# The first load of x in two transfers, one of 16 partitions and one of the other 112, in a fused residual add and layer normalisation

## The chip, the cores and the metric

One core of a Trainium2 chip. The metric is the time of one execution on the device in microseconds (us), the median of several. The profile's span is 1.3 us shorter than the time of the same run (236.7 for 238.0 us before).

Some terms: SBUF is the on-chip memory, with 128 partitions. A load is cut into packets, here one for each partition that it writes, and 16 DMA engines move them; it has landed when each of the 16 has reported its share (so 144 packets for a load of all partitions: the trace of before has 4464 for 31 transfers, 496 of them of 4 bytes). A row, of a load, is what it writes in one partition: one packet.

## The reference

```python
# x, residual: (16, 1024, 512) float32; gamma, beta: (512,)
z = x + residual
mean = np.mean(z, axis=-1, keepdims=True)
var = np.var(z, axis=-1, keepdims=True)
return gamma * (z - mean) / np.sqrt(var + eps) + beta
```

That is 16384 rows of 512 numbers; 33.55 MB each of x, of the residual and of the result.

## The kernel before

Every partition holds 128 of the rows. The plan names the transfers in the order in which the SP queue issues them: x0+8 is rows 0 to 7 of each partition, 16 KB per partition. POOL adds x and the residual in place, ACT takes mean and variance, DVE normalises into the buffer of x, and SP stores from there.

```python
PLAN = """
x0+8 r0+8 x8+8 r8+8 x16+16 r16+16 x32+16 r32+16 x48+16
o0+16 r48+16 o16+16 x64+16 ...
"""
EARLY = 2
# ... cut ...
def dram(t, lo, n):                 # 128 pieces of n rows, 32 KB apart in memory
    b0 = lo - lo % BLOCK
    v = t[P * b0 : P * (b0 + BLOCK), :].rearrange("(p j) d -> p j d", p=P)
    return v[:, lo - b0 : lo - b0 + n, :].rearrange("p a b -> p (a b)")
# ... cut ...
def move(out, in_, s):
    i = nc.sync.dma_start(out=out, in_=in_).then_inc(s, 16)
    if len(first) < EARLY:
        first.append(i.ins)         # these are put ahead of the start-up barrier
# ... cut: for each word of the plan ...
        if kind == "x":
            # ... wait for the store that frees the place ...
            move(part(zbuf, Z_ROWS, lo, n), dram(xf, lo, n), sx[loads_x.index((lo, n))])
# ... cut: POOL ...
            while landed[key] < len(loads) and loads[landed[key]][0] < lo + n:
                nc.gpsimd.wait_ge(s[landed[key]], 16)
```

## Time and profile before

| | before |
|---|---|
| time, median of the first 3 runs | 238.26 us (238.25 to 238.43) |
| span of the profile | 236.7 us |
| DMA queue's packets, share of 16 engines' span | 99.4% |
| ACT, DVE, POOL busy | 78%, 75%, 61% |
| one 16 KB packet, undisturbed | 0.611 us |
| first add starts | 12.29 us |

The first row carries the result, the third says what bounds it: 16 DMA engines whose packets fill 99.4% of the span. The lines behind this table are shown in the prediction.

### The profile page before, as it was taken

To read this page: it belongs to the slowest core of one execution; us is meant where nothing else is said; L and a number is where in the kernel's file an instruction comes from. 1 tells how busy PE (TensorE), PEld (TensorE's weight loads), DVE (VectorE), ACT (ScalarE), POOL (GpSimd) and SP (SyncE) were. 2 spreads that over 40 slices of the span, in tenths; PEclk is the share of its full clock that TensorE was granted. 3 is DMA by queue.
4 is the path that set the end of the run, shared out by engine and by line. 5 is a ranking of instruction groups with operands and counts; after the bars stand their busy time and mean duration, and the time that the engine had idled before them with its cause. 6 is when DMAs were issued, how large, how long until landed. Compare 5 with 4: busy or idle time off the path is not lost.

```text
span 236.7 us, 1000 instructions
## 1 busy us (share of the span) xinstructions
PE 3.8 (2%) x4; PEld 1.2 (0%) x4; DVE 177.2 (75%) x290; ACT 183.8 (78%) x545; POOL 144.0 (61%) x36
## 2 busy tenths in 40 slices
PE   0600000000000000000000000000000000000000
PEld 0100000000000000000000000000000000000000
DVE  0001999629999999599980999809999999999950
ACT  2019997299999996999909998099999999999600
POOL 0098920999799307993079920899799798800000
DMA  8999999999999999999999999999999999999997
GB/s 310 443 426 432 426 443 443 443 443 443 410 388 443 443 443 432 426 393 432 443 443 443 443 438 421 415 421 432 429 424 435 426 432 440 439 432 443 438 390 324
DMA packets 4469, 100.68 MB, mean 425 GB/s; under 512 B 498, under 2 KB 498, under 8 KB 500
## 3 DMA queue, kind: packets, MB, share of 16 engines
q1 hardware_dynamic: 4464, 100.67, 99.4%
q14 instruction: 1, 0.01, 0.0%
q10 hardware_dynamic: 4, 0.00, 0.0%
HBM read 67.11 MB, written 33.55 MB: 425 GB/s over the span
## 4 chain that ended last, share of the span: by engine, by line
ACT 48%; DMA 35%; POOL 6%; DVE 4%; issue 1%; SPq 1%; ACTq 0%; DVEq 0%; POOLq 0%
DMA rbuf<-in_residual_dram 35%; ACT junk_s L211 25%; ACT junk_m L201 21%; POOL rbuf L178 6%; DVE zbuf L239 3%; ACT std L220 2%; DVE zbuf L253 1%; SPq L140 1%; DVE rstd L247 0%; ACTq L194 0%; DVEq L231 0%; POOLq L175 0%; ACTq L199 0%; ACTq L195 0%
## 5 line engine op out<-in xcount | busy, mean ns | idle before, releaser
L178 POOL TENSOR_TENSOR rbuf<-zbuf,rbuf 128x2048 f32<-128x2048 f32 x32 | 143.7, 4521 | 62.2 <-DMA rbuf<-in_residual_dram 60.0
L239 DVE SCALAR_TENSOR_TENSOR zbuf<-rbuf,nm,gamma_p 128x512 f32<-128x512 f32 x128 | 87.1, 743 | 47.8 <-ACT std L220 47.8
L201 ACT ACTIVATE junk_m<-rbuf 128x512 f32<-128x512 f32 x128 | 74.2, 580 | 34.0 <-POOL rbuf L178 33.7
L211 ACT ACTIVATE junk_s<-rbuf,nm 128x512 f32<-128x512 f32 x128 | 88.8, 694 | 1.0
L253 DVE SCALAR_TENSOR_TENSOR zbuf<-zbuf,rstd,beta_p 128x512 f32<-128x512 f32 x128 | 87.1, 744 | 1.1
L211 ACT ACTIVATION_READ_ACCUMULATOR junk_s<-rbuf,nm 128x1 f32 x128 | 23.9, 187 | 0.0
L201 ACT ACTIVATION_READ_ACCUMULATOR junk_m<-rbuf 128x1 f32 x128 | 23.8, 186 | 0.0
L220 ACT ACTIVATE std<-ssq,eps_t 128x4 f32<-128x4 f32 x32 | 9.5, 297 | 1.0
L247 DVE RECIPROCAL rstd<-std 128x4 f32<-128x4 f32 x32 | 5.5, 171 | 0.0
L192 ACT ACT_TABLE_LOAD x1 | 1.3, 1283 | 2.7 <-PEq L60 2.7
L131 PE MATMUL gamma_p<-gb_row,ones 1*128 1x512 f32 x2 | 2.0, 1122 | 6.6 <-DMA gb_row<-in_gamma_dram 6.6
L131 PE MATMUL beta_p<-gb_row,ones 1*128 1x512 f32 x2 | 1.9, 1056 | 0.0
L126 DVE MEMSET ones<- 1x128 f32 x1 | 0.2, 165 | 2.0 <-PEq L60 2.0
L131 PEld LDWEIGHTS beta_p<-gb_row,ones 1*128 1x128 f32 x2 | 0.7, 332 | 1.0 <-DMA gb_row<-in_beta_dram 0.5
L131 PEld LDWEIGHTS gamma_p<-gb_row,ones 1*128 1x128 f32 x2 | 0.5, 306 | 6.6 <-issue 6.6
L294 POOL MEMSET const-float32-0.0<- 128x1 f32 x1 | 0.1, 98 | 0.2 <-issue 0.2
L294 POOL MEMSET const-bfloat16-1.0<- 128x1 bf16 x1 | 0.1, 101 | 0.0
L294 POOL MEMSET const-uint8-127<- 128x1 uint8 x1 | 0.1, 101 | 0.0
L294 POOL MEMSET const-float32-1.0<- 128x1 f32 x1 | 0.1, 98 | 0.0
L127 DVE MEMSET eps_t<- 128x1 f32 x1 | 0.1, 59 | 0.0
## 6 DMA issues: line engine op xcount, KB each, us to landing
zbuf<-in_x_dram SPq DMA_DIRECT2D x6, 4096.0 KB, 28.9
rbuf<-in_residual_dram SPq DMA_DIRECT2D x6, 4096.0 KB, 21.2
out_dram<-zbuf SPq DMA_DIRECT2D x6, 4096.0 KB, 31.0
zbuf<-in_x_dram SPq DMA_DIRECT2D x4, 2048.0 KB, 14.9
rbuf<-in_residual_dram SPq DMA_DIRECT2D x4, 2048.0 KB, 14.0
out_dram<-zbuf SPq DMA_DIRECT2D x3, 2048.0 KB, 22.5
out_dram<-zbuf SPq DMA_DIRECT2D x2, 1024.0 KB, 10.0
gb_row<-in_gamma_dram ACTq DMA_DIRECT2D x1, 2.0 KB
```

The source lines that it names most:

```text
L126: nc.vector.memset(ones[:, :], 1.0).then_inc(s_const, 1)
L131: nc.tensor.matmul(dest[:, :], ones[:, :], gb_row[:, k * D : (k + 1) * D], start=True, stop=True).then_inc(s_pe, 1)
L140: i = nc.sync.dma_start(out=out, in_=in_).then_inc(s, 16)
L178: nc.gpsimd.tensor_tensor(out=z, in0=part(zbuf, Z_ROWS, lo, n), in1=z, op=ALU.add).then_inc(s_sum[lo // TURN % R_TURNS], 1)
L192: act.preload_act_table_set("sqrt_and_others")
L201: i = act.activation(out=junk_m[k][:, :], in_=part(rbuf, R_ROWS, r, 1), func=ACT.Identity, scale=-inv_d, accum_out=column(nm, r),)
L211: i = act.activation(out=junk_s[k][:, :], in_=part(rbuf, R_ROWS, r, 1), func=ACT.Square, bias=column(nm, r), accum_out=column(ssq, r),)
L220: act.activation(out=column(std, rows[0], TURN), in_=column(ssq, rows[0], TURN), func=ACT.Sqrt, bias=eps_t[:, 0:1], scale=inv_d,).then_inc ...
L239: dve.scalar_tensor_tensor(out=part(zbuf, Z_ROWS, r, 1), in0=part(rbuf, R_ROWS, r, 1), scalar=column(nm, r), in1=gamma_p[:, :], op0=ALU.ad ...
L247: dve.reciprocal(out=column(rstd, rows[0], TURN), in_=column(std, rows[0], TURN)).then_inc(s_rstd[j], 1)
L253: i = dve.scalar_tensor_tensor(out=z, in0=z, scalar=column(rstd, r), in1=beta_p[:, :], op0=ALU.mult, op1=ALU.add,)
L294: nc = _bacc.Bacc("TRN2", target_bir_lowering=False, num_devices=1)
```

## The change

Its intent is not written down; its shape suggests one: a first transfer of 16 partitions would give each of the 16 DMA engines one row at once, so that all start early.

```diff
+AHEAD = 16
...
-            move(part(zbuf, Z_ROWS, lo, n), dram(xf, lo, n), sx[loads_x.index((lo, n))])
+            cuts = (0, AHEAD, P) if lo == 0 else (0, P)
+            for a, b in zip(cuts, cuts[1:]):
+                move(
+                    part(zbuf, Z_ROWS, lo, n)[a:b, :],
+                    dram(xf, lo, n)[a:b, :],
+                    sx[loads_x.index((lo, n))],
+                )
...
-                nc.gpsimd.wait_ge(s[landed[key]], 16)
+                twice = key == "x" and landed[key] == 0
+                nc.gpsimd.wait_ge(s[landed[key]], 32 if twice else 16)
```

Since EARLY stays 2, both pieces of x go ahead of the barrier and the first residual load behind it.

## The prediction

The sum came to 1.83 + 0.2 - 0.25 + 0.01 = +1.8 us, so 240.06, and 239.9 us with a little off for the rivals. The 1.83 of step 4 is three more row times of 0.611 us: the author assumed that a first row takes four of them if the 16 rows go to partitions 0 to 15. The 0.2 of step 5 is a guess between nothing and one row time more for the seven rows of each engine. The 0.15 of step 3 is a guess from the measured spread of 0.47 us. In the paragraph on range and chances, 239.6 to 240.8 us, and the word contention, stand for the losses of steps 4 and 5.

> **What bounds the kernel now.** I read the summary by slices first, because the change touches only a load and the question is whether loads are the bound at all. In the page of the kernel before, the rows of section 2 for the DMA engines and their rate, the rows of section 3, and the bytes:
>
> ```profile
> DMA  8999999999999999999999999999999999999997
> GB/s 310 443 426 432 426 443 443 443 443 443 410 388 443 443 443 432 426 393 432 443 443 443 443 438 421 415 421 432 429 424 435 426 432 440 439 432 443 438 390 324
> q1 hardware_dynamic: 4464, 100.67, 99.4%
> HBM read 67.11 MB, written 33.55 MB: 425 GB/s over the span
> ```
>
> The 16 DMA engines are busy from the first slice to the last (each slice is 236.7/40 = 5.9 us), and the queue's packets fill 99.4% of the 16 engines' span. No compute engine comes near: DVE 75%, ACT 78%, POOL 61%. The chain of waits names ACT for 48% of the span, but every long wait of POOL in it ends on a load, and ACT waits on POOL. What matters is that ACT's waits cost the DMA engines nothing: the queue never runs dry.
>
> Then the packet records of the trace. The kernel moves 100.66 MB, 6.29 MB for each engine, or 384 rows of 16 KB. An undisturbed 16 KB packet takes 611 ns (26.8 GB/s per engine, 429 GB/s for 16), one of 32 KB 1213 ns. All packets of q1 together, divided by 16, are 235.2 us. The first packet starts at 1.02 us and the last one ends at 236.1, its landing following at 236.6. So there is next to no idle time after the start: **the span is the start, plus the packets' time, plus about half a microsecond of last landing.** Anything that makes the DMA engines lose time at the start moves the end by the same amount, since nothing later has slack on that side; anything that moves only compute does not.
>
> The stretches of the beginning, with DMA share and GB/s as the last two columns (bytes are put down to where a packet starts, so the first stretches are lumpy):
>
> ```profile
> 0.00:1.00 1.00, 0.00 (x0) 0.00 (x0) 0.00 (x0) 0.00 (x0) 0.20 (x4) 1.00 0.00 0
> 1.00:1.50 0.50, 0.00 (x0) 0.00 (x0) 0.00 (x0) 0.00 (x0) 0.00 (x0) 1.00 2.47 524
> 1.50:2.00 0.50, 0.00 (x0) 0.00 (x0) 0.00 (x0) 0.00 (x0) 0.00 (x0) 1.00 0.00 0
> 2.00:2.50 0.50, 0.00 (x0) 0.00 (x0) 0.17 (x2) 0.00 (x0) 0.00 (x0) 1.00 0.90 360
> 3.00:4.00 1.00, 0.00 (x0) 0.00 (x0) 0.00 (x0) 0.99 (x1) 0.00 (x0) 1.00 1.01 426
> ```
>
> Nothing moves in the first microsecond; the 16 first packets, one per engine, start between 1.02 and 1.49 (mean 1.20), last 1.02 to 1.37 us instead of 0.611, and end at 2.43 on average. From there each engine runs one packet per 0.61 us. The whole possible gain is in this corner: the 0.2 us by which the mean start trails the first one, and the 0.6 us by which each first packet is too long.
>
> The issues on the SP queue, from the timeline:
>
> ```profile
> 0.00 0.38 SPq L140 DMA_DIRECT2D zbuf<-in_x_dram  x1
> 0.43 0.42 SPq L140 DMA_DIRECT2D rbuf<-in_residual_dram  x1
> 1.92 0.33 SPq L140 DMA_DIRECT2D zbuf<-in_x_dram  x1
> 12.29 8.95 POOL L178 TENSOR_TENSOR rbuf<-zbuf,rbuf 128x2048 f32<-128x2048 f32 x2 [11.85 <-DMA rbuf<-in_residual_dram]
> ```
>
> Two issues stand ahead of the start-up barrier; the next is at 1.92. The first add waits for the residual's load until 12.29, long after x's own (last share at 7.31 us).
>
> [...]
>
> **The change part by part.**
>
> 1. *One issue more, and order.* The instruction listing of the changed kernel shows that only SP's list differs, with 31 rows for 30. The two transfers ahead of the barrier are now both of x; the first residual load moves behind the barrier. It is issued near 1.92 instead of 0.43, and everything behind it slips by one issue, 0.33 to 0.51 us. x's rows keep each engine occupied until about 6.7 us (mean end of the first packet 2.43 + 7 x 0.611), so a residual issue at 1.92 with about 1.0 us to its first packet is ready by 3: nothing starves. Cost 0. One more transfer also means 16 more completion packets of 9 ns, one per engine: 0.01 us.
>
> 2. *POOL's wait for 32 instead of 16*: same wait, ends when both landed. Cost 0.
>
> 3. *Earlier first packets.* [...] the mean start moves from 1.20 to about 1.05: a gain of 0.15 us, 0.4 at most for the last-starting engine. The first start itself, 1.02 after the issue's beginning, may move forward if it waits for the whole issue (0.38 us), by up to 0.3; I give that a third and count 0.1. Gain about 0.25.
>
> 4. [...] each first packet ends 1.83 us later, near 4.25 less the gain of step 3, so 4.0. [...] Cost 1.83 us.
>
> 5. [...] a further 0 to 0.6 us, partly hidden as engines that are ahead go on to the residual. I count 0.2.
>
> Sum: 1.83 + 0.2 - 0.25 + 0.01 = +1.8 us on the DMA path and, as the path has no slack, on the time: 238.26 + 1.8 = 240.06. I take a little off for rivals below: **239.9 us**.
>
> **The rivals.**
>
> *The early start wins.* [...] only step 3 is left: 237.8 to 238.2. For it speaks the shape of the change: 16 is just the number that gives each engine one row, as somebody would choose who knows the engine count. [...] I give it 20%.
>
> *Hidden anyway.* The first add doesn't need x before 12.29, and x lands at 7.31. A delay of x alone would be hidden from compute. But the residual's packets stand in the same engines behind x's, and the bound is the DMA queue, not compute. For "same to 0.1 us" the two effects would have to cancel: 10%.
>
> *A poor split of 112.* If 112 rows ran on eight engines (14 rows each), these would have 8.6 us of work; six rows more than before are 3.7 us late on half the engines[...]. Then 242 to 244. [...] 4%.
>
> *Late residual.* If the residual's issue slipped to beyond 5 us through the barrier, the engines would run dry. It would take 3 us more than the 1.92 seen; nothing in the change touches the barrier.
>
> **Range and chances.** [...] 239.6 to 240.8 (step 4 less step 3 alone is +1.6, with the whole of step 5 +2.2, and 0.2 for the spread of runs); contention of half the size 239.0; the early start alone 238.0. Eight times in ten: 238.0 to 240.8. 2% is 4.77 us; no rival but the poor split comes near, and the largest possible gain is the idle 1.02 us and the 0.6 us of slow first packets, under 2%. So faster 0.005, within 97.5%, slower 0.02.
>
> **What would show it.** In the changed kernel's packet records, the first 16 packets should last about 3.0 us and not 1.2, and end near 4.0; x's last share should land near 9 instead of 7.3, the first add start near 14 instead of 12.29, the first slice fall from 310 GB/s to about 190 (1.8 us x 429 GB/s = 0.77 MB less, over 5.9 us), and all other slices keep their rates. The first starts should lie within 0.2 us. Step 4 is wrong if the first packets stay under 1.6 us; step 1 if a gap opens on the DMA engines before 7 us; step 5 if packets of the second transfer stay at 0.611 throughout or run far over it. The prediction as a whole fails if the first add comes earlier than 12.29 and the time falls below 238.

## More of the kernel before

One more view is needed for the comparison, the beginning in stretches of 2 us (columns: stretch and length, busy time and instructions of PE, PEld, DVE, ACT, POOL, granted clock, DMA share, GB/s), of the kernel before:

```profile
0.00:2.00 2.00, 0.00 (x0) 0.00 (x0) 0.00 (x0) 0.00 (x0) 0.20 (x4) 1.00 0.62 131
2.00:4.00 2.00, 0.00 (x0) 0.00 (x0) 0.17 (x2) 1.28 (x1) 0.00 (x0) 1.00 0.94 393
4.00:6.00 2.00, 0.00 (x0) 0.00 (x0) 0.00 (x0) 0.00 (x0) 0.00 (x0) 1.00 0.95 402
6.00:8.00 2.00, 1.37 (x2) 0.83 (x3) 0.00 (x0) 0.00 (x0) 0.00 (x0) 1.00 1.08 460
8.00:10.00 2.00, 2.00 (x3) 0.33 (x1) 0.00 (x0) 0.00 (x0) 0.00 (x0) 1.00 1.05 451
```

From 2 us on the rate is that of the whole run (425 GB/s); a packet's bytes count where it starts, so single stretches lie a little over or under.

## The result, and the profile after

241.6 us (241.32 to 241.71, 4 runs) against 238.28 us before: ratio 1.0137 (95% interval 1.0122 to 1.0152). A ratio is the mean time of one kernel's fast runs over that of the other's in the same rounds, so it is not quite the ratio of the medians quoted. The time lies outside the range of 238.0 to 240.8 us, and the loss of 3.3 us is twice the 1.6 us forecast. The direction was right, the place half right, the size wrong.

The page of the changed kernel, the rows that answer to those in the prediction:

```profile
GB/s 197 323 431 421 464 437 437 431 431 437 421 426 410 437 421 431 437 437 437 437 437 437 437 431 426 437 431 421 412 431 426 431 429 442 433 437 437 437 393 311
q1 hardware_dynamic: 4480, 100.67, 99.3%
HBM read 67.11 MB, written 33.55 MB: 419 GB/s over the span
```

The first two slices carry the loss: 197 for 310 and 323 for 443 GB/s. The first one alone is near what was forecast (190 is written there; the sum beside it, 0.77 MB over 5.9 us off 310, gives 179); the second one was to stay as it was. In microseconds of the engines' full rate of 429 GB/s: (310 - 197) x 5.9 us / 429 = 1.55 us in the first, (443 - 323) x 6.0 / 429 = 1.68 us in the second, together 3.2. The DMA queue is as "busy" as before, 99.3%: **a packet counts as busy for as long as it lasts**, at 0.9 to 1.7 us as at 0.61, so the share can't show this loss, only the rate can.

The same stretches of 2 us in the changed kernel:

```profile
0.00:2.00 2.00, 0.00 (x0) 0.00 (x0) 0.00 (x0) 0.00 (x0) 0.20 (x4) 1.00 0.68 139
2.00:4.00 2.00, 0.00 (x0) 0.00 (x0) 0.17 (x2) 1.28 (x1) 0.00 (x0) 1.00 0.98 172
4.00:6.00 2.00, 0.00 (x0) 0.00 (x0) 0.00 (x0) 0.00 (x1) 0.00 (x0) 1.00 0.98 279
6.00:8.00 2.00, 0.00 (x0) 0.00 (x0) 0.00 (x0) 0.00 (x0) 0.00 (x0) 1.00 1.10 312
8.00:10.00 2.00, 0.51 (x1) 0.50 (x2) 0.00 (x0) 0.00 (x0) 0.00 (x0) 1.00 1.01 280
10.00:12.00 2.00, 2.00 (x3) 0.61 (x2) 0.00 (x0) 0.00 (x0) 0.00 (x0) 1.00 0.89 377
12.00:14.00 2.00, 1.24 (x2) 0.00 (x0) 0.00 (x0) 0.00 (x0) 0.00 (x0) 1.00 0.96 410
14.00:16.00 2.00, 0.00 (x0) 0.00 (x0) 0.00 (x0) 0.00 (x0) 0.13 (x1) 1.00 1.02 434
```

There are two parts: one stretch at 172 GB/s, then six microseconds at 279 to 312, and from about 11 us the full rate again. The packet records put figures to it. Sorted by start in groups of 16, one packet for each engine, the mean durations are (us):

| packet of each engine | 1 | 2 | 3 | 4 | 5 | 6 | 7 | 8 | 9 | 10 |
|---|---|---|---|---|---|---|---|---|---|---|
| before | 1.23 | 0.64 | 0.63 | 0.62 | 0.63 | 0.61 | 0.61 | 0.61 | 0.61 | 0.61 |
| after | 1.24 | 1.68 | 0.99 | 0.92 | 0.86 | 0.91 | 0.94 | 0.97 | 0.92 | 0.62 |

The first is as long as before, the second 1.04 us longer, the third to ninth 2.19 us longer in sum. Together 3.2 us, which is the loss. By count, the first packet of each engine is of the 16 rows, the next seven are of the 112, and the ninth is of the residual. A landing comes about one packet after the last packet's end in these records: x0 landed at 7.31 us in before, where the eighth packets end at 6.76 on average and the ninth at 7.38, and the 16 rows at 4.25 in the changed kernel, where the first packets end at 2.39 and the second at 4.08. So a slow row seems to show one packet late, and the second packet is read here as the price of the 16 rows and the third to ninth as that of the 112, which experiments 7 and 10 measure apart. The timeline and the landings of the changed kernel (issue to landing, by size):

```profile
0.00 0.86 SPq L143 DMA_DIRECT2D zbuf<-in_x_dram  x2
1.92 0.35 SPq L143 DMA_DIRECT2D rbuf<-in_residual_dram  x1
15.87 4.49 POOL L188 TENSOR_TENSOR rbuf<-zbuf,rbuf 128x2048 f32<-128x2048 f32 x1 [15.43 <-DMA rbuf<-in_residual_dram]
```

```profile
zbuf<-in_x_dram SPq DMA_DIRECT2D x1, 1792.0 KB, 10.5
zbuf<-in_x_dram SPq DMA_DIRECT2D x1, 256.0 KB, 4.3
```

The 16 rows, 256 KB, need 4.3 us to land, the other 112 are there at 10.9 us (all of x0 at 7.3 before), the first add starts 3.6 us later, and everything after it is shifted as a whole: the last store lands 3.3 us later.

### The profile page after: what moved, and what is told of

Its sections match the earlier page's. It is cut to its first block, busy times and chain, and to the rows that moved or that the text cites. A ratio compares the mean times of both kernels' runs of the same rounds, so it can differ in the third digit from the quotient of the medians.

```text
span 240.0 us, 1001 instructions
## 1 busy us (share of the span) xinstructions
PE 3.7 (2%) x4; PEld 1.1 (0%) x4; DVE 177.2 (74%) x290; ACT 183.8 (77%) x545; POOL 144.0 (60%) x36
## 3 DMA queue, kind: packets, MB, share of 16 engines
q1 hardware_dynamic: 4480, 100.67, 99.3%
## 4 chain that ended last, share of the span: by engine, by line
ACT 48%; DMA 36%; POOL 6%; DVE 4%; issue 1%; SPq 1%; ACTq 0%; DVEq 0%; POOLq 0%
DMA rbuf<-in_residual_dram 36%; ACT junk_s L221 25%; ACT junk_m L211 21%; POOL rbuf L188 6%; DVE zbuf L249 3%; ACT std L230 2%; DVE zbuf L263 1%; SPq L143 1%; DVE rstd L257 0%; ACTq L204 0%; DVEq L241 0%; POOLq L185 0%; ACTq L209 0%; ACTq L205 0%
```

## The experiments

P is the theory that the loss lies in which partitions are written: rows to some sets of partitions, here called crowded, hold each other up (collide, in the expectations), rows to others don't. Its rivals name the number or the size of the transfers, the start, the barrier and the reading side. Which sets are crowded, and by how much, the author assumed before each run from a layout that no run of this case shows. P's figures (mostly the first ones given) read as bets. Each edit is given against the changed kernel ("after") or the kernel before; the times of before are those of the same rounds.

**1. Is it the residual load that left the opening?** Against after:

```diff
-EARLY = 2
+EARLY = 3
```

> The changed kernel with three transfers ahead of the barrier instead of two, so that the first residual load is again issued at about 1 us and not at 1.92. [...] no change, 241.6 us, first sixteen packets 1.2 us, the others of x0 0.8 to 1.05 us. Rival, the residual load that left the opening is the cost: back to about 238.3 us.

Measured: 241.3 us against 238.13, ratio 1.0144 (1.0127 to 1.0161). The residual is issued at 0.90 us, ahead of the barrier again, and nothing is won; second packets 1.70 us, the next 0.79 to 1.03. The rival falls.

**2 and 3. Cuts of the same kind on other partitions.** Against after, for 64+64 `AHEAD = 64`; for 32+64+32:

```diff
-            cuts = (0, AHEAD, P) if lo == 0 else (0, P)
+            cuts = (0, 32, 96, P) if lo == 0 else (0, P)
...
-                nc.gpsimd.wait_ge(s[landed[key]], 32 if twice else 16)
+                nc.gpsimd.wait_ge(s[landed[key]], 48 if twice else 16)
```

> The first load cut at partition 64, four rows per engine in each piece. [...] all eight rows take 1.22 us instead of 0.611: 8 x 0.61 = 4.9 us more, 243.2 us. Rival, that it is the small piece of 16 or the odd number 7 of rows that costs: 238.3 to 238.6 us, packets at 0.611. Rival, a fixed cost per further transfer: 241.6.

> The first load in three pieces: partitions 0-31, 32-95, 96-127. [...] 4 x 0.61 = 2.4 us more, 240.7 us, less than the two pieces of 64 although there is one transfer more. Rival, number of transfers or size of the pieces: more than 64+64, or twice the change's 3.3 us, 244.9 us.

Measured: 64+64 243.0 us, ratio 1.0207 (1.019 to 1.0224), +4.9 us as expected, though the exact agreement is partly luck: 0.47 us of it is a later start (the first packets start at 1.67 us on average, for 1.20), and the packets themselves lose 4.4; 32+64+32 240.38 us, ratio 1.0099 (1.0083 to 1.0116), +2.3 us (the bet was 1.22 us a row in the outer pieces, two rows per engine in each, and 0.611 in the middle one). The three pieces cost half of the two. Stretches of the kernel with 64+64, then of that with 32+64+32:

```profile
2.00:4.00 2.00, 0.00 (x0) 0.00 (x0) 0.17 (x2) 0.71 (x1) 0.00 (x0) 1.00 1.08 238
4.00:6.00 2.00, 0.00 (x0) 0.00 (x0) 0.00 (x0) 0.57 (x1) 0.00 (x0) 1.00 0.84 172
8.00:10.00 2.00, 0.00 (x0) 0.00 (x0) 0.00 (x0) 0.00 (x0) 0.00 (x0) 1.00 1.00 206
```

```profile
2.00:4.00 2.00, 0.00 (x0) 0.00 (x0) 0.17 (x2) 0.88 (x1) 0.00 (x0) 1.00 1.15 254
4.00:6.00 2.00, 0.00 (x0) 0.00 (x0) 0.00 (x0) 0.41 (x1) 0.00 (x0) 1.00 0.82 336
8.00:10.00 2.00, 1.95 (x2) 0.50 (x2) 0.00 (x0) 0.00 (x0) 0.00 (x0) 1.00 0.85 254
```

The middle lines matter most: at 4 to 6 us both kernels have a 64-partition transfer in flight, four rows per engine (64 rows on 16), at 172 GB/s for partitions 0 to 63 and at 336 where 32 to 95 have taken over. (Either side of it the three pieces run near 254, their two outer ones being crowded.) In the packets it is sharper: 1.13 to 1.28 us each in 64+64, against fourth to sixth packets of 0.66, 0.61 and 0.62 us in the middle piece. **The same number of rows per engine and the same size of packet, at half or at full speed depending on which partitions they go to.** That excludes the number of transfers and their size as the cause.

**4. The other order.** Against after: `AHEAD = 112`.

> The two pieces in the other order, 112 partitions and then 16. [...] the collisions of the seven-row blocks stay (2 us by the packets of the changed kernel[...]) and so does the sixteen-row piece, now behind it: 240.3 to 241.6 us; the first seven packets per engine run at 0.75 to 1.0 us and the eighth at 1.6 to 2.4. Rival, that the small piece costs only because it comes first, before the engines have anything else: 238.3 to 239.

Measured: 241.74 us, ratio 1.0152 (1.0135 to 1.0169): +3.6, a little above the bracket. The pieces are now partitions 0 to 111 and 112 to 127. The seven packets of the 112-row piece come first: they end at 8.13 us on average, against 6.15 before, so this piece alone loses 1.98 us. The rest comes with the 16 rows behind it: packets eight and nine take 1.52 and 1.57 us, 1.9 us too much together, where 1.6 to 2.4 us had been expected of the eighth alone. The small piece costs without being the first.

**5. Two transfers, all partitions.** Against after:

```diff
-            cuts = (0, AHEAD, P) if lo == 0 else (0, P)
+            cuts = (0, D, n * D) if lo == 0 else (0, n * D)
...
-                    part(zbuf, Z_ROWS, lo, n)[a:b, :],
-                    dram(xf, lo, n)[a:b, :],
+                    part(zbuf, Z_ROWS, lo, n)[:, a:b],
+                    dram(xf, lo, n)[:, a:b],
```

> The first load again in two transfers, but both on all 128 partitions: one of 2 KB and one of 14 KB per partition. [...] 238.3 us, give or take 0.3 (16 x 8 more small packets). Rival, the second transfer itself or the residual load behind the barrier costs: 240 to 241.6 us.

Measured: 238.26 us, ratio 1.0011 (0.9988 to 1.0033). A second transfer and a residual behind the barrier are free. So is the early start that a small first piece might bring: nothing is gained either.

**6. The cut at a later load.** Against after: `if lo == 8` for `if lo == 0`, and POOL's double wait at the second load.

> The cut of 16 and 112 at the second load of x (rows 8 to 15) instead of the first, 2 us later in the stream. [...] the same eight packets per engine are slow wherever they lie: +2.6 to +3.4 us, about 241.3 us. Rival, a matter of the start[...]: below +0.5 us, 238.3 to 238.8 us.

Measured: 242.32 us, ratio 1.0177 (1.0158 to 1.0195). The rival, that it is a matter of the start, falls. But +4.2 us is over the expected 3.4. The packets say where most of the rest lies: those of the 112 rows lose 2.3 us, about as in the changed kernel (2.19), but the first two, which take 1.38 and 1.58 us, lose 1.75, where the changed kernel's loses 1.04. That is close to the 1.9 us of experiment 4: 16 such rows cost more behind other rows than at the very start. The first residual load, ahead of the cut, is also whole only at 13.4 us instead of 12.15. The cause of the difference stays open.

**7 and 8, 11 and 12. The 16 rows measured by themselves.** Against before, an extra load at the very start into a free place; EARLY is 3, and x48 waits for it. For partitions 0 to 15, with 16 KB rows:

```diff
+    extra = sem("extra")
...
         if kind == "x":
+            if lo == 0:
+                move(part(zbuf, Z_ROWS, 48, 8)[0:16, :], dram(xf, 0, 8)[0:16, :], extra)
+            if lo == 48:
+                nc.sync.wait_ge(extra, 16)
```

The spread variant has `[32:96:4, :]` as destination; the doubled ones `(zbuf, Z_ROWS, 48, 16)` and `dram(xf, 0, 16)`, 32 KB rows.

> The kernel before with one load more at the very start, 16 rows of 16 KB to partitions 0 to 15 of a place that is free then[...]. One row per engine costs 0.61 us if no engine waits for another. [...] 4 x 0.61 = 2.44 us: 240.7 us. What the packets of the changed kernel suggest (first two packets 1.0 us over): 0.6 + 1.0 = 1.6 us, 239.9. Rival, [...]: 238.9.

> The same extra load, same 16 source rows, to partitions 32, 36, ... 92[...]. [...] 0.61 us, 238.9 us, with no packet over 0.65 us after the first ones. Rival, the source side or a transfer of 16 partitions as such: the same as the extra load to partitions 0 to 15.

> As the extra load to partitions 0 to 15, with rows of 32 KB. One row per engine is 1.21 us. [...] 4 x 1.21 = 4.85 us, less the 0.7 us[...]: about +4.1 us, 242.3 us. [...] +1.2, 239.3 us.

> As the extra load to partitions 32, 36 ... 92, with rows of 32 KB. [...] +1.2 us and the later first issue seen in the 16 KB run (0.35 us): 239.4 to 239.8 us; it must lie 2.5 to 3 us below the load to partitions 0 to 15. Rival, transfers of 16 partitions are slow[...]: the same as that one.

| extra load | time | ratio (95%) |
|---|---|---|
| partitions 0-15, 16 KB | 239.83 us | 1.0071 (1.0054, 1.0088) |
| 32, 36 ... 92, 16 KB | 239.64 us | 1.0054 (1.0037, 1.0071) |
| partitions 0-15, 32 KB | 242.36 us | 1.0177 (1.0163, 1.019) |
| 32, 36 ... 92, 32 KB | 240.04 us | 1.0079 (1.0065, 1.0093) |

The loads to partitions 0 to 15 cost 1.7 and 4.2 us. That is what was expected from the packets of the changed kernel (1.6) and then from the first of these runs (4.1: 4.85 less the 0.7 us by which 1.7 lies under 2.44); four row times, 4 x 0.611 and 4 x 1.213, had said 2.44 and 4.85. The spread ones cost 1.5 and 1.9, which is more than the 0.6 and 1.2 expected; with 16 KB rows the two times can hardly be told apart, and with 32 KB rows they lie 2.3 us apart, where 2.5 to 3 had been called for. The times alone would not have decided; the traces do. From the issue to the landing, the loads to 0-15 and to the spread partitions, 16 KB rows, one line from each kernel:

```profile
zbuf<-in_x_dram SPq DMA_DIRECT2D x1, 256.0 KB, 4.2
```

```profile
zbuf<-in_x_dram SPq DMA_DIRECT2D x1, 256.0 KB, 2.9
```

And with 32 KB rows, again 0-15 first:

```profile
zbuf<-in_x_dram SPq DMA_DIRECT2D x1, 512.0 KB, 6.6
```

```profile
zbuf<-in_x_dram SPq DMA_DIRECT2D x1, 512.0 KB, 3.6
```

Doubling the rows, by 16 KB each, adds 2.4 us to the landing at partitions 0 to 15, which is four times the 0.61 us of an undisturbed 16 KB packet, and 0.7 us at the spread ones, which is little more than once. What the spread loads lose otherwise has two visible parts in their profiles. Both have their first packet at 1.37 us, since their first issue takes 0.59 us instead of 0.38. And both have a dip near 69 us (the spread 16 KB one another near 127 us) in which nearly every engine's 32 KB packet is 0.1 to 1.2 us too long: beyond 14 us, their packets exceed the undisturbed ones by 1.5 and 1.7 us per engine, those of the loads to 0-15 by 0.7. Why, I don't know; before has one such dip, 16 packets at 68.5 to 68.9 us that take 1.3 to 1.9 us instead of 1.213, after none. By the profiles, one for each kernel, the dip shows only where no early load was much crowded: between 60 and 140 us such long packets cost 0.4 to 1.25 us per engine in before and in experiments 5, 8, 12 and 13, 0.25 in 14, and 0.04 or less in all the others. So a time against before can make crowding look some 0.4 us cheaper than it is, and the spread loads some 0.8 us dearer.

**9. Is it the reading side?** Against after, the source of the first load packed, 16 KB from row to row instead of 32 KB; the result is wrong on purpose (relative error 0.25):

```diff
-                    dram(xf, lo, n)[a:b, :],
+                    (xf[0 : P * n, :].rearrange("(p a) d -> p (a d)", p=P)
+                     if lo == 0 else dram(xf, lo, n))[a:b, :],
```

> The changed kernel, 16 and 112 partitions, but the source rows of the first load packed end to end (16 KB pitch in memory instead of 32 KB; the result is wrong on purpose). [...] the destination partitions are the same, so nothing changes: +3.0 to +3.4 us over before, the second to eighth packets at 0.8 to 1.0 us. Rival, the reading side of memory makes the rows slow: packets and time change, towards 0.61 us and 238.3 us.

Measured: 241.49 us, ratio 1.0148 (1.0132 to 1.0163); second packets 1.67 us, the next 0.83 to 0.97. So the pitch of the source rows does not matter here, as P says.

**10. The 112 rows by themselves.** As the extra load of 7, with `[16:128, :]` on both sides.

> The kernel before with one load more at the start, 112 rows of 16 KB to partitions 16 to 127 of a place that is free then. Without collisions seven rows per engine cost 7 x 0.611 = 4.28 us: 242.4 us. [...] what the swapped order showed (first seven packets end 1.98 us late): 4.3 + 2.0 = 6.3 us, 244.4 us. [...]

Measured: 244.4 us, ratio 1.0276 (1.0259 to 1.0293): +6.3 us, of which 7 x 0.611 = 4.28 are the rows' own time. Beyond that the piece costs 2.0 us, the same as in experiment 4.

**13 and 14. How much hangs on two partitions?** The 112 rows cost 2.0 us, and the runs so far don't show how. So the smallest contrast: an extra load of 64 rows as in 7, to `[32:96, :]` (aligned), the partitions that ran at 0.61 to 0.66 us per packet in experiment 3, against the same two partitions further, `[34:98, :]` (shifted). That the shifted rows would collide in a few places only was the assumption.

> The kernel before with an extra load at the start: 64 rows of 16 KB to partitions 32 to 95[...]. [...] four rows per engine at 0.611, +2.44 us, 240.6 us (up to 241.0 if the first issue is late as it was for the strided load), all packets after the first at 0.61 to 0.65 us. Rival, any transfer on fewer than 128 partitions is slow: 1.5 times that or more, 241.9 or over.

> The same shifted by two partitions, 34 to 97[...]. If a collision slows only those who meet: within 0.3 us of the unshifted load in the mean of the engines' packets, up to 0.6 to 1.2 us in the time if the late engine is the one that ends last. If it slows all engines: +0.6 us or more in the mean of the packets, all of the third and fourth packets near 0.9 us.

Measured: aligned 241.12 us, ratio 1.0134 (1.0114 to 1.0155), second to fourth packets 0.65, 0.64 and 0.62 us; +3.0 us, of which 2.44 are the rows' own and 0.37 the late first packet (1.39 us); it has the dip too, near 70 us. Shifted 242.41 us, ratio 1.0173 (1.016 to 1.0187). Stretches of the aligned, then of the shifted one:

```profile
4.00:5.00 1.00, 0.00 (x0) 0.00 (x0) 0.00 (x0) 0.84 (x1) 0.00 (x0) 1.00 0.94 393
5.00:6.00 1.00, 0.00 (x0) 0.00 (x0) 0.00 (x0) 0.00 (x0) 0.00 (x0) 1.00 1.07 459
6.00:7.00 1.00, 0.00 (x0) 0.00 (x0) 0.00 (x0) 0.00 (x0) 0.00 (x0) 1.00 1.00 428
```

```profile
4.00:5.00 1.00, 0.00 (x0) 0.00 (x0) 0.00 (x0) 0.84 (x1) 0.00 (x0) 1.00 1.02 311
5.00:6.00 1.00, 0.00 (x0) 0.00 (x0) 0.00 (x0) 0.00 (x0) 0.00 (x0) 1.00 0.96 377
6.00:7.00 1.00, 0.00 (x0) 0.00 (x0) 0.00 (x0) 0.00 (x0) 0.00 (x0) 1.00 0.79 330
```

Neither side was quite right. The seventh packets end 0.33 us later on average, close to "only those who meet". But of the 16 fifth packets, one for each engine, three take 1.1 to 1.5 us and the other thirteen 0.74 to 0.81 too, instead of 0.61: nearly all are held up, most of them for one packet and by less. From issue to landing, the aligned, then the shifted load:

```profile
zbuf<-in_x_dram SPq DMA_DIRECT2D x1, 1024.0 KB, 5.3
```

```profile
zbuf<-in_x_dram SPq DMA_DIRECT2D x1, 1024.0 KB, 7.1
```

The first of its 16 shares is there as early as in the aligned kernel (4.78 and 4.63 us), the last 1.9 us later. **What falls behind stays behind**: x0 and the first residual land 1.7 us later than in the aligned kernel, and three microseconds before the last packet of all ends, only five engines still have one, 16 in the aligned kernel (the queue's share is 98.4% for 99.3%). So the time grows by more than the mean, 1.3 us by the medians. A few late engines can thus cost more than their mean; that the 2.0 us of the 112 rows come about in this way is not shown.

No version beat the kernel before; the two transfers on all partitions equal it.

## Why the prediction was wrong, point by point

- **The bound, and that a start delay of the DMA engines moves the end one for one: right.** The packet records lose 3.2 us before 11 us and the time grows by 3.3.
- **Step 1 (order, one issue more, cost 0) and step 2 (the wait for 32): right.** Experiments 1 and 5. (The traces have 32 transfers for 31, by 4480 and 4464 packets; the prediction's 31 rows for 30 are of a listing that is not on record.)
- **Step 3 (earlier first packets, a gain of 0.25): wrong, and small.** The mean first start moved from 1.20 to 1.15 us and they still spread over 0.32 us (1.02 to 1.35), where all were to start within 0.2. In the three other runs that open with 16 such rows to partitions 0 to 15 (1, 7 and 9) they spread over 0.29, 0.34 and 0.47, for 0.47 before: that the spread goes with the number of rows is not borne out. The gain is 0.05 at most.
- **Step 4 (the rows to partitions 0 to 15 take four row times, a cost of 1.83): the place right, the size too large for a piece that comes first.** The extra load of experiment 7 measures 1.70 - 0.61 = 1.1 us beyond its own row, and the changed kernel's second packets show 1.04. With 32 KB rows the cost beyond the own row is 4.2 - 1.2 = 3.0 instead of 3.64: again 0.6 to 0.7 us are missing. Behind other rows they are not: there 16 rows to neighbouring partitions lose 1.9 us (experiment 4, at 112 to 127) and 1.75 (experiment 6, at 0 to 15) in the packets, near the 1.83 of the sum. So the term that failed is "each first packet ends 1.83 us later": a first packet of the kernel before already takes 1.23 us instead of 0.61; whether part of the crowding passes under these 0.6 us is not shown. The view to check was named wrong, too: first packets stay at 1.24 us, and it is the second that becomes long. (In experiment 7 the second packets end at 4.00 us on average while the 16 rows land only at 4.16, so here too the slow rows show one packet late.) By the test that step 4 set itself, "wrong if the first packets stay under 1.6 us", it would have been given up, and wrongly.
- **Step 5 (seven rows per engine, 0.2): this is the step that failed.** It measured 2.0 us, twice (experiments 4 and 10), and 2.19 in the packets of the changed kernel, which run at 0.86 to 0.99 us: "far over" 0.611, as its own test had it. I had put its worst case at the time of eight rows where seven took theirs, 0.6 us, from an assumed layout. The runs don't show how the loss comes about; experiment 14 shows only that a shift by two partitions makes some packets 1.1 to 1.5 us long and thirteen others 0.74 to 0.81.
- The sum with measured terms: 1.1 + 2.0 - 0.05 = 3.1 us, against 3.3 measured. The two errors of step 4 and 5 partly cancelled, which is luck. The signs named with them missed as well: x whole at 10.9 us and not near 9, the first add at 15.87 and not near 14.
- **The rivals.** The early start: gone, with 0.05 us. Hidden anyway: no. A poor split of 112 (eight engines; its sum left out the first piece's row, so it would have been 15 rows and 4.3 us late, not 14 and 3.7): no, the queue has 4480 packets for 4464, so both pieces have the 16 completions of a transfer on 16 engines. Late residual: no.

What is shown: the destination partitions decide (experiments 2, 3, 13, 14, and with the same source rows 7 against 8 and 11 against 12), not the number of transfers, the barrier, or the pitch of the source (1, 5, 9). Not shown: which engine writes which partition, since the packet records don't name engines, and why partitions 32 to 95 take 64 rows at full speed (0.61 to 0.66 us per packet) and 0 to 63 at half (1.13 to 1.28). Open: how the 2.0 us of step 5 come about; why the 16 rows cost some 0.7 us less at the very start than behind other rows; the dip near 68 us; and why the two opening issues take 0.55 to 0.61 us each in some kernels (64+64, the spread loads, 64 extra rows), which delays the first packet by 0.3 to 0.4 us.

## What to carry to other kernels

When the DMA engines bound a kernel, as here (99.4% of their span), try a cut along the bytes of a partition before one along the partitions: for the first load of 2 MB, the former cost nothing here (238.26 us for 238.13) and the latter 2.3 to 4.9 us. If partitions must be cut, measure the pieces alone, since the choice of partitions decides: 64 rows to 32 to 95 ran at 0.61 to 0.66 us per packet, to 0 to 63 at 1.13 to 1.28, and two partitions beside the good place cost 1.3 us. And judge such a change by the rate and by the length of single packets: the busy share of the DMA queue was 99% in both kernels.
